# Start places of matmul operands: one fixed pair, or a spread over 32 and 64 places

## The chip, the cores and the metric

The kernel runs on one core of one Trainium2 chip. The time is the device time of one execution in microseconds (us). A core has five engines with queues of their own: TensorE (PE, matmuls; its weight loads are shown apart as PEld), VectorE (DVE), ScalarE (ACT), GpSimd (POOL) and SyncE (SP, which here issues the DMAs). They work out of an on-chip memory of 128 partitions; a place in it is told here in 32-bit words along the partition.

## The reference

One step of a decoder layer, for a prompt of 256 tokens and 8 sequences of 4 new tokens each. The 288 tokens go through the same weights. Three branches (convolution, stick-breaking attention, attention over a memory) are gated, added and projected with `w_o`; then comes the feed-forward part, which is half of the work:

```python
merged = gates[:, :, 0] * y_conv + gates[:, :, 1] * y_sb + gates[:, :, 2] * y_mem
x = x + merged @ p['w_o']                                    # 2048 x 2048
h2 = rms_norm(x, p['g_mlp'])
x = x + jnp.square(jax.nn.relu(h2 @ p['w_up'])) @ p['w_down']   # 2048 x 8192, 8192 x 2048
```

All of it is in 32-bit floats.

## The kernel before

Features lie along the partitions and the 288 tokens along the columns. A product of 32-bit precision is made of three fast ones: each operand is split into a high part, rounded to the format `float32r`, and a low part, the rest. An output tile of 128 features by 288 tokens is the sum, over 16 blocks of 128 input features, of high times high, high times low and low times high: 48 matmuls of 288 columns. The weights are the stationary operand (128 columns, loaded before each matmul) and the activations the moving one.

The weights come in 504 slabs of 128 x 1024 words, one DMA each (L285). ACT rounds a slab into a buffer of the pool `wh` (L307), DVE puts the difference into one of `wl` (L318); both pools have four buffers of 1088 words, 64 more than a slab. `shifted` chooses the column in the buffer at which the slab begins: 0 for the first 16 slabs, 5 (`SHIFT`) for all others. `products` (L538) runs through a slab: first the high weights with the high and the low part of each activation block in turn, then the low weights with the high parts, 24 matmuls. Two slabs make an output tile of a product with 2048 input features; the last 256 slabs are the feed-forward part's.

The activations lie in two kinds of places. `Acts` takes two buffers of 320 words from pool `a`, one for the high and one for the low part, and begins at word 4 (`AHEAD`) in both; `hx`, the input of the first half, and `h2`, the input of `w_up`, are of this kind. The homes (`make_homes`) are cut from ten buffers of pool `k4` of 1024 words, three to a buffer, 320 words (`APART`) from one to the next, and from two buffers of pool `s`: 32 in all, a high and a low one for each of 16 blocks. They begin at word 36 (`HOME`) of their section. `merged`, the input of `w_o`, is in the homes, and then, for each of the four quarters of the feed-forward part, the 16 blocks that `w_up` produces and `w_down` reads. In the compiled program the buffers of `a` begin 16 words past a multiple of 64, and those of `k4`, `s`, `wh` and `wl` 48 past. With the columns above, each moving operand of L538 begins 20 words past a multiple of 64, and its weights 53 past (48 in the first 16 slabs, which L591 multiplies, with the roles exchanged: there the slab is the moving operand, 512 columns at a time). The names of the profile leave out numbers: `k` is `k4`.

The small attention products (`three`, L917 to L919) read operands that begin at the buffers' own first column or a multiple of 128 behind it.

The order of all engines' work is found when the program is built: a planner (`Order`) steps jobs, each with an engine, an estimated time and buffers that it needs, and issues what can start first. A matmul counts as 0.131 us there. In the feed-forward part TensorE runs the tiles of `w_up` (`up_tile`: DVE takes the relu out of the sum, POOL squares, ACT and DVE make the high and the low home) and then those of `w_down` (`down_tile`), for each of the quarters.

Of the kernel before, what the change touches and what calls it, by code (L numbers as in the profile page):

```python
# [8 lines left out]
F32R = mybir.dt.float32r  # L9
# [6 lines left out]
P = 128  # L16
D_MODEL = 2048
KT = D_MODEL // P
# [4 lines left out]
T = NP + NS  # L23
# [14 lines left out]
N_SLABS = 504  # L38
# [37 lines left out]
class Order:  # L76
# [31 lines left out]
    def give(self, pool, n=1):  # L108
        self.pools[pool] += [self.now.ready] * n
# [45 lines left out]
def dve(n, *flags, **take):  # L155
    return Ask("DVE", 0.18 + n / 920.0, flags, **take)


def act(n, *flags, **take):
    return Ask("ACT", 0.22 + n / 1200.0, flags, **take)  # L160


def pool(n, *flags, **take):
    return Ask("POOL", 0.3 + n / 420.0, flags, **take)


def pe(us, *flags, **take):
    return Ask("PE", us, flags, **take)


def sp(*flags, **take):
    return Ask("SP", 0.45, flags, **take)


APART = 320
AHEAD, HOME = 4, 36
PAD = 64
GRP = 32
SHIFT = 5
MM = 0.131  # L180
MM_MEM = 0.226

# [2 lines left out]
def tile_decoder_step(ctx: ExitStack, tc: tile.TileContext, xT, memT, wall, cvec, kmat, ptab,  # L185
# [23 lines left out]
    def tl(p, shape, dt=F32):  # L209
        cnt[0] += 1  # L210
        return pools[p].tile(shape, dt, tag=p, name=f"{p}_{cnt[0]}")
# [48 lines left out]
    def col(c):  # L260
        return cv[:, c:c + 1]
# [9 lines left out]
    class Slab:  # L271
        def __init__(self, parts):
            self.parts = parts
            self.landed = [Flag() for _ in range(parts)]
            self.split = [Flag() for _ in range(parts)]
# [11 lines left out]

    def shifted(p, s):
        n = 0 if s < 2 * KT // 2 else SHIFT
        return tl(p, [P, SLAB + PAD], F32R)[:, n:n + SLAB]  # L290

    def due(s):
# [4 lines left out]
    def cast_weights():  # L297
        todo = [(0, 0), (1, 0), (0, 1), (1, 1)] + [(s, i) for s in range(2, N_SLABS) for i in range(slabs[s].parts)]
        for s, i in todo:
            sl = slabs[s]  # L300
            n = SLAB // sl.parts
            cast_at[0] = s
            yield act(n, sl.landed[i], **({} if i else {"w": 1}))
            if i == 0:
                sl.h = shifted("wh", s)
            c = slice(i * n, (i + 1) * n)
            nc.scalar.copy(sl.h[:, c], sl.raw[:, c])  # L307
            sl.split[i].cast = order.now.ready
            add(sub_part(s, i), lambda s=s: 0 if due(s) - order.free["DVE"] < 5.0 else 4.5)

    def sub_part(s, i):
        sl = slabs[s]
        n = SLAB // sl.parts
        yield dve(n, late=Order.HOP + 0.1)
        if i == 0:
            sl.l = shifted("wl", s)
        c = slice(i * n, (i + 1) * n)
        nc.vector.tensor_sub(sl.l[:, c], sl.raw[:, c], sl.h[:, c].bitcast(F32))  # L318
        done(sl.split[i])
        if i == sl.parts - 1:  # L320
            give("wr")
# [5 lines left out]
    class Acts:  # L327


        def __init__(self, n=T):  # L330
            c = slice(AHEAD, AHEAD + n) if n == T else slice(32, 32 + n)
            self.h, self.l = tl("a", [P, APART], F32R)[:, c], tl("a", [P, APART], F32R)[:, c]
            self.flag = Flag()

    hm, hx = [None] * KT, [None] * KT
# [208 lines left out]
    def products(ps, uses, acts, first=True, last=True, n=T):  # L544
# [6 lines left out]
        for i in range(0, len(todo), STEP):  # L551
            part = todo[i:i + STEP]
            yield pe(len(part) * MM, *sl.split, *{a.flag for _, _, a, _ in part})
            if i == 0 and first:
# [45 lines left out]
    def conv_products(evacs):  # L600
# [8 lines left out]
        for k2, o in turns:  # L609
# [9 lines left out]
            for i in range(2):  # L619
                todo.append((sl.l, slice(i * 512 + o * P, i * 512 + (o + 1) * P), "h", 2 * k2 + i))  # L620
            yield pe(6 * MM, *sl.split, hx_in[2 * k2], hx_in[2 * k2 + 1])
            if o == 0:
# [704 lines left out]
    def make_homes():  # L1327
        yield sp(*conv_done, *osb_in, k4=bufs["k4"], s=bufs["s"])
        parts = []
        for _ in range(bufs["k4"]):  # L1330
            x = tl("k4", [P, 1024], F32R)
            parts += [x[:, HOME + i * APART:HOME + i * APART + T] for i in range(3)]
        for _ in range(bufs["s"]):
            parts.append(tl("s", [P, 512], F32R)[:, HOME:HOME + T])
        for j in range(KT):
            homes.append(Home(parts[2 * j], parts[2 * j + 1]))
        done(homes_in)
# [45 lines left out]
    x1, h2 = [None] * KT, [None] * KT  # L1383
# [4 lines left out]
    def out_tile(j):  # L1388
        res = []
        here = Flag()  # L1390

        def load():
            yield sp(t=1)
            res.append(tl("t", [P, T]))
            nc.sync.dma_start(res[0], xT[:, j, :])
            here.at = order.landed(147) + 1.0

        def evac(ps):
            yield dve(T, here, a=3)
            x = x1[j] = tl("a", [P, T])  # L1400
            nc.vector.tensor_add(x, ps, res[0])
            give("pm")
            a = h2[j] = Acts()
            yield act(T)
            nc.scalar.mul(a.h, x, col(C_GMLP + j))
            yield dve(T)
            nc.vector.scalar_tensor_tensor(a.l, x, col(C_GMLP + j), a.h.bitcast(F32), op0=ALU.mult, op1=ALU.subtract)
            done(h2_in[j])
            a.flag = h2_in[j]
            yield act(T)  # L1410
            if j == 0:
                sq_sum.append(res[0])
            nc.scalar.activation(res[0], x, AF.Square)  # L1413
            if j:
                yield pool(T)
                nc.gpsimd.tensor_add(sq_sum[0], sq_sum[0], res[0])  # L1416
                give("t")
            if j == KT - 1:
                done(sums_2)
        return load, evac  # L1420
# [110 lines left out]
    with tc.manual_schedule():  # L1531
        add(loads(), 1.0)
        add(cast_weights(), lambda: 0 if due(cast_at[0]) - order.free["ACT"] < 6.0 else 4.5)
        add(mem_norm(), 0.6)
        add(x_norm(), 0.6)
        add(main(), 20.0)
        add(conv_norm(), 8.0)
        add(read_pages(), 4.0)
        add(make_homes(), 1.0)
        order.run()  # L1540
# [157 lines left out]
```

## Time and profile before

| what | value |
|---|---|
| time, median of 2 runs | 1616.84 us (1616.59 to 1617.10) |
| the profiled execution | 1617.72 us, its span 1615.9 us |
| TensorE busy, share of the span | 1610.4 us, 100% |
| VectorE, ScalarE, GpSimd busy | 978.3, 752.6, 139.6 us |
| DMA | 310.25 MB, mean 192 GB/s |

The span is from the first instruction of the program to the end of the last. A group of instructions is shown with its line, engine, operation, the tiles it writes and reads (`pm<-a,wh` is a matmul into `pm` with the moving operand from `a` and the weights from `wh`), its count, the total and the mean time of one, and what ended the idle time before it. The chain of waits follows the work that ended last back to the start. A row of a window gives its length, the busy time (and count) of the engines asked for, the granted share of TensorE's clock, and the DMAs' share and rate. Matmuls overlap in their pipeline, so the time of one (292 ns) is not what it costs; the distance from start to start is. A row of the timeline begins with the start in us and the time.

### The profile page before, as it was taken

How to read it: one execution, taken by the hardware profiler on the slowest of the kernel's cores; microseconds unless marked ns; L12 is line 12 of the kernel's file. 1: busy time of each engine (PE TensorE's matmuls, PEld its weight loads, DVE VectorE, ACT ScalarE, POOL GpSimd, SP SyncE). 2: the span in 40 equal slices, each digit the busy share in tenths (PEclk: the TensorE clock that was granted, in tenths of full speed). 3: DMA queues.
4: the chain of work that ended last, by engine and by line, in shares of the span. 5: the costliest groups of instructions: out<-in, count | busy, mean ns of one | idle time of the engine just before them, and what ended most of it. 6: DMA issues, size and time to landing. Idle time of an engine off the chain costs nothing.

```text
span 1615.9 us, 30749 instructions
## 1 busy us (share of the span) xinstructions
PE 1610.4 (100%) x12638; PEld 1592.4 (99%) x12638; DVE 978.3 (61%) x1503; ACT 752.6 (47%) x1078; POOL 139.6 (9%) x106
## 2 busy tenths in 40 slices
PE   9999999999999999999999999999999999999999
PEld 7999999999999999999999999999999999999999
DVE  7889888877777655655555544555445554455443
ACT  8856877654334534444443333333333333333332
POOL 0020000000000000002222100121002210022100
PEclk9999999999999999999999999999999999999999
DMA  9887778987755555466655555555555555555562
GB/s 326 231 198 267 201 256 237 323 225 271 220 170 166 173 169 170 151 195 191 193 171 167 170 170 169 168 170 171 169 170 170 170 170 169 171 167 169 180 194 95
DMA packets 127200, 310.25 MB, mean 192 GB/s; under 512 B 40018, under 2 KB 49618, under 8 KB 127058
## 3 DMA queue, kind: packets, MB, share of 16 engines
q1 hardware_dynamic: 126770, 307.98, 61.2%
q8 instruction: 99, 1.62, 0.4%
q10 hardware_dynamic: 288, 0.29, 0.1%
q14 instruction: 43, 0.35, 0.1%
HBM read 296.99 MB, written 6.32 MB: 188 GB/s over the span
## 4 chain that ended last, share of the span: by engine, by line
PE 97%; DVE 1%; DMA 1%; issue 0%; ACT 0%; SPq 0%; DVEq 0%; ACTq 0%
PE pm L538 91%; PE pm L591 3%; DMA wr<-in_wall 1%; PE pa L538 1%; PE pl L1090 1%; DVE wl L318 1%; PE pl L1274 0%; PE pa L917 0%; PE pa L919 0%; PE pa L918 0%; PE pl L1104 0%; DVE a L770 0%; PE pa L1214 0%; PE pa L1250 0%; ACT wh L307 0%
## 5 line engine op out<-in xcount | busy, mean ns | idle before, releaser
L307 ACT CAST wh<-wr 128x1024 fp32r<-128x1024 f32 (+1 forms) x520 | 529.2, 1022 | 643.3 <-PE pm L538 570.6
L318 DVE TENSOR_TENSOR wl<-wr,wh 128x1024 fp32r<-128x1024 f32 (+1 forms) x520 | 618.2, 1193 | 192.6 <-ACT wh L307 189.6
L538 PE MATMUL pm<-a,wh 128*128 128x288 f32 x5184 | 733.9, 292 | 0.0
L538 PEld LDWEIGHTS pm<-a,wh 128*128 128x128 f32 x5184 | 695.2, 188 | 1.4 <-issue 1.0
L538 PE MATMUL pm<-a,wl 128*128 128x288 f32 x2592 | 394.9, 292 | 0.0
L538 PEld LDWEIGHTS pm<-a,wl 128*128 128x128 f32 x2592 | 358.0, 188 | 0.0
L538 PE MATMUL pm<-k,wh 128*128 128x288 f32 x2400 | 338.0, 292 | 0.0
L538 PEld LDWEIGHTS pm<-k,wh 128*128 128x128 f32 x2400 | 321.6, 188 | 0.0
L538 PE MATMUL pm<-k,wl 128*128 128x288 f32 x1200 | 181.8, 292 | 0.0
L538 PEld LDWEIGHTS pm<-k,wl 128*128 128x128 f32 x1200 | 165.4, 188 | 0.0
L1430 POOL TENSOR_TENSOR t<-t 128x288 f32<-128x288 f32 x64 | 96.7, 1510 | 599.2 <-DVE t L1427 599.2
L1444 DVE TENSOR_TENSOR a<-a,pm 128x288 f32<-128x288 f32 x64 | 29.0, 454 | 122.7 <-PE pm L538 122.7
L1427 DVE SCALAR_TENSOR_TENSOR t<-pm,rx 128x288 f32<-128x288 f32 x64 | 29.3, 457 | 92.1 <-PE pm L538 92.1
L1433 ACT CAST k<-t 128x288 fp32r<-128x288 f32 x60 | 26.0, 433 | 126.0 <-POOL t L1430 126.0
L1346 DVE TENSOR_TENSOR t<-pm,rx 128x288 f32<-128x288 f32 x48 | 22.0, 458 | 71.8 <-PE pm L538 71.8
L1435 DVE TENSOR_TENSOR k<-t,k 128x288 fp32r<-128x288 f32 x60 | 28.0, 466 | 59.4 <-ACT k L1433 59.4
L770 DVE SCALAR_TENSOR_TENSOR a<-a,cv,a 128x256 f32<-128x256 f32 x120 | 59.5, 496 | 1.4
L1416 POOL TENSOR_TENSOR t<-t,t 128x288 f32<-128x288 f32 x15 | 21.9, 1462 | 413.9 <-ACT t L1413 413.9
L591 PE MATMUL pm<-wh,a 128*128 128x512 f32 x128 | 34.8, 392 | 0.5 <-ACT wh L307 0.5
L538 PE MATMUL pm<-s,wh 128*128 128x288 f32 x160 | 33.8, 292 | 0.0
L591 PEld LDWEIGHTS pm<-wh,a 128*128 128x128 f32 x128 | 24.1, 190 | 6.5 <-ACT wh L307 1.6
L538 PEld LDWEIGHTS pm<-s,wh 128*128 128x128 f32 x160 | 25.6, 188 | 0.0
(181 smaller groups left out, 707.7 us busy)
## 6 DMA issues: line engine op xcount, KB each, us to landing
wr<-in_wall SPq DMA_DIRECT2D x488, 512.0 KB, 3.7
wr<-in_wall SPq DMA_DIRECT2D x32, 256.0 KB, 5.1
k<-in_kpool SPq DMA_DIRECT2D x32, 256.0 KB, 5.9
k<-in_vpool SPq DMA_DIRECT2D x32, 256.0 KB, 5.9
k<-in_mkc SPq DMA_DIRECT2D x8, 512.0 KB, 8.9
k<-in_mvc SPq DMA_DIRECT2D x8, 512.0 KB, 8.2
t<-in_xT SPq DMA_DIRECT2D x16, 144.0 KB, 3.7
out_yT<-a SPq DMA_DIRECT2D x16, 144.0 KB, 1.9
```

Source lines behind the costliest of these rows:

```text
L307: nc.scalar.copy(sl.h[:, c], sl.raw[:, c])
L318: nc.vector.tensor_sub(sl.l[:, c], sl.raw[:, c], sl.h[:, c].bitcast(F32))
L538: nc.tensor.matmul(ps, w, a, start=(first and i == 0), stop=(last and i == len(todo) - 1))
L591: nc.tensor.matmul(ps[m], y[:, m * P:(m + 1) * P], z[:, w], start=(k == 0 and j < 2), stop=(k == KT - 1 and j in (4, 5)))
L770: nc.vector.scalar_tensor_tensor(c[:, :NP], up[:, k:k + NP], w, c[:, :NP], op0=ALU.mult, op1=ALU.add)
L1346: nc.vector.tensor_mul(g, ps, rx)
L1416: nc.gpsimd.tensor_add(sq_sum[0], sq_sum[0], res[0])
L1427: nc.vector.scalar_tensor_tensor(r, ps, 0.0, r2, op0=ALU.max, op1=ALU.mult)
L1430: nc.gpsimd.tensor_mul(r, r, r)
L1433: nc.scalar.copy(a.h, r)
L1435: nc.vector.tensor_sub(a.l, r, a.h.bitcast(F32))
L1444: nc.vector.tensor_add(x1[j], x1[j], ps)
```

## The change

Operands of the feed-forward part no longer begin at one common place. The weights of the output tile number 16 c + f (quarter c, tile f, in `w_up` and `w_down` alike) begin at column 27 (16 c + f) mod 64 of their buffers, so that all 64 values occur. The 32 buffers of `h2` begin at 11 i mod 32, with i = 0 to 31 through the high and low parts in turn. The 32 homes begin at (11 i + 32 k) mod 64 of their section, where k is the section's number in its buffer; that gives 32 different places of the 64. The homes hold `merged` too, so that the product with `w_o` reads its moving operand from the new places, with its weights at 5 as before. All else, the other users of `Acts` among it, stays at word 4 and shift 5; no buffer changes its size, and no instruction is added or taken away.

```diff
-AHEAD, HOME = 4, 36
+AHEAD, HOME = 4, 0
+FF0 = N_SLABS - 4 * 4 * KT

     def shifted(p, s):
         n = 0 if s < 2 * KT // 2 else SHIFT
+        if s >= FF0:
+            c, i = divmod(s - FF0, 4 * KT)
+            n = 27 * (c * KT + i // 2 % KT) % 64
         return tl(p, [P, SLAB + PAD], F32R)[:, n:n + SLAB]

-        def __init__(self, n=T):
-            c = slice(AHEAD, AHEAD + n) if n == T else slice(32, 32 + n)
-            self.h, self.l = tl("a", [P, APART], F32R)[:, c], tl("a", [P, APART], F32R)[:, c]
+        def __init__(self, n=T, at=(AHEAD, AHEAD)):
+            c, d = (slice(x, x + n) if n == T else slice(32, 32 + n) for x in at)
+            self.h, self.l = tl("a", [P, APART], F32R)[:, c], tl("a", [P, APART], F32R)[:, d]

             x = tl("k4", [P, 1024], F32R)
-            parts += [x[:, HOME + i * APART:HOME + i * APART + T] for i in range(3)]
+            for i in range(3):
+                at = i * APART + (11 * len(parts) + 32 * i) % 64
+                parts.append(x[:, at:at + T])
         for _ in range(bufs["s"]):
-            parts.append(tl("s", [P, 512], F32R)[:, HOME:HOME + T])
+            at = 11 * len(parts) % 64
+            parts.append(tl("s", [P, 512], F32R)[:, at:at + T])

-            a = h2[j] = Acts()
+            a = h2[j] = Acts(at=[11 * (2 * j + x) % 32 for x in range(2)])
```

## The prediction

> **What bounds the kernel now.** I read the page first: its shares of busy time, its row of granted clock, and its chain of waits.
>
> ```profile
> span 1615.9 us, 30749 instructions
> PE 1610.4 (100%) x12638; PEld 1592.4 (99%) x12638; DVE 978.3 (61%) x1503; ACT 752.6 (47%) x1078; POOL 139.6 (9%) x106
> PEclk9999999999999999999999999999999999999999
> PE 97%; DVE 1%; DMA 1%; issue 0%; ACT 0%; SPq 0%; DVEq 0%; ACTq 0%
> PE pm L538 91%; PE pm L591 3%; DMA wr<-in_wall 1%; PE pa L538 1%; PE pl L1090 1%; DVE wl L318 1%; PE pl L1274 0%; PE pa L917 0%; PE pa L919 0%; PE pa L918 0%; PE pl L1104 0%; DVE a L770 0%; PE pa L1214 0%; PE pa L1250 0%; ACT wh L307 0%
> ```
>
> TensorE is on the chain for 97% of the span, and 91% of it is one line, the product loop L538. The clock is granted in full in all slices (a 9 is 90% or more; a row below says 1.00), so the time of this line is a count of matmuls times the spacing of their starts. Next comes the chain in order of time, for its last pieces.
>
> ```profile
> 422.81 3.70 PE pl L1090 x128
> 426.52 1185.81 PE pm L538 x9120
> 1612.33 0.02 issue
> 1612.35 0.46 DVE a L1444
> ```
>
> From 426.5 us to the end nothing interrupts the products: 9120 matmuls in 1185.81 us, 130.02 ns each, for 288 columns. The busy time of this line by stretches says the same: TensorE stands still for 0.69 us out of 1086.50, and the weight loads run beside the matmuls without a gap.
>
> ```profile
> 526.50:1613.00 1086.50, 1085.81 (x8353) 1085.59 (x8351) 1.00 0.54 170
> ```
>
> So the sum has one kind of term: a change in the 130.0 ns, times the matmuls that it concerns. The other engines stand off this chain, which the groups by line and shape show.
>
> ```profile
> L318 DVE TENSOR_TENSOR wl<-wr,wh 128x1024 fp32r<-128x1024 f32 x488 | 597.3, 1226 | 190.1 <-ACT wh L307 187.2 <-ACT t L1413 1.5 <-DVE t L461 0.4
> L307 ACT CAST wh<-wr 128x1024 fp32r<-128x1024 f32 x488 | 510.8, 1048 | 638.9 <-PE pm L538 570.6 <-issue 29.0 <-DMA wr<-in_wall 20.9
> L318 DVE TENSOR_TENSOR wl<-wr,wh 128x512 fp32r<-128x512 f32 x32 | 21.0, 686 | 2.5 <-ACT wh L307 2.3
> L307 ACT CAST wh<-wr 128x512 fp32r<-128x512 f32 x32 | 18.4, 612 | 4.5 <-DMA wr<-in_wall 4.2
> L538 PEld LDWEIGHTS pm<-a,wh 128*128 128x128 f32 x5184 | 695.2, 188 | 1.4 <-issue 1.0 <-ACT s L986 0.4
> L591 PEld LDWEIGHTS pm<-wh,a 128*128 128x128 f32 x128 | 24.1, 190 | 6.5 <-ACT wh L307 1.6
> ```
>
> ACT, which makes each weight slab's high part, waits 570.6 us for TensorE to free a buffer: it is the one that is early.
>
> **What the change touches.** It adds, removes and reorders no instruction, wait or transfer. The planner's costs stay, so the order stays; the buffers keep their sizes, so they keep their addresses. SP's and POOL's queues hold what they held. Only start columns move. Of the instructions that touch them:
>
> The casts and subtractions that write the weights. Before, the first slabs (512 columns at a time) are written at shift 0 and all others (1024) at shift 5. In the rows above 512 more columns cost ACT 1048 − 612 = 436 ns and DVE 1226 − 686 = 540 ns, less than the first 512 with their fixed part, so no dearness of an odd place stands out, and odd the places of the feed-forward weights are already. I set the cost at nothing. Were it 10% either way, it would be 123 ns for a DVE subtraction of 1226 that comes once in 24 × 130.0 = 3120 ns; TensorE hides it, with ACT's wait as the measure of the slack. If that cover were gone, it would be 256 × 0.12 = 31 us.
>
> The small evacuations into h2 and into the homes (64 + 16 on ACT, as many on DVE): the same reasoning, and none ends a wait of TensorE.
>
> The matmuls and weight loads. Feed-forward slabs are 504 − 248 = 256, with 24 matmuls each: 6144, or 799 us of the 1185.81. In them the moving operand and the weights move. In the output product with w_o, 16 tiles of 48 = 768 matmuls read `merged` out of the same homes; there the moving operand alone moves.
>
> **What a place costs.** Before, every product of L538 has the same pair of places: moving operands 20 words past a multiple of 64 (16 + 4 in `a`, 48 + 36 in the homes), weights 53 past (48 + 5). Their difference is 33. So the trace has the price of one pair out of the 32 × 64, and for others I go to matmuls on other lines. In the memory products (L591) both operands stand at 48, a difference of 0, with 512 columns. In the attention products of 256 columns two kinds stand: `pa<-a,a`, both at 16 (difference 0), and `pa<-s,a`, moving at 48 and weights at 16 (difference 32). The chain from 10 to 50 us, and the timeline at two such groups, the matmul behind each included:
>
> ```profile
> 9.94 40.12 PE pm L591 x177
> ```
>
> ```profile
> 157.27 0.28 PE L917 MATMUL pa<-a,a 128*128 128x256 f32 x1
> ...
> 157.86 0.28 PE L919 MATMUL pa<-a,a 128*128 128x256 f32 x1
> 157.98 0.30 PE L538 MATMUL pm<-a,wh 128*128 128x288 f32 x1
> ```
>
> ```profile
> 177.51 0.28 PE L917 MATMUL pa<-s,a 128*128 128x256 f32 x1
> ...
> 178.35 0.28 PE L918 MATMUL pa<-s,a 128*128 128x256 f32 x1
> 178.47 0.28 PE L919 MATMUL pa<-s,a 128*128 128x256 f32 x1
> 178.59 0.27 PE L1250 MATMUL pa<-s,a 128*128 128x128 f32 x1
> ```
>
> The first gives 40.12 / 177 = 226.7 ns for 512 columns. The second has six matmuls from 157.27 to 157.98: 118.3 ns. The third has nine from 177.51 to 178.59: 120.0 ns. Starts are rounded to 10 ns, so these two are good to 1.7 and 1.1 ns. At difference 0 a column costs (226.7 − 118.3) / 256 = 0.423 ns. For 288 columns that makes 118.3 + 32 × 0.423 = 131.8 ns at difference 0, and 120.0 + 13.5 = 133.5 ns at difference 32. The pair of now, at 130.0, is the cheapest of the three, by 1.8 and 3.5 ns.
>
> The change replaces this one pair by a spread over all of them. The mean of the three known prices is 131.8, 1.8 ns over now. I take 1.5 ns, a little less, because pairs as odd as the present one come up often among the new ones and the two dear ones both begin on round places. The bounds: above, all at 133.5, +3.5 ns. Below, a matmul that costs its columns alone, 288 × 0.423 = 121.8 ns, −8.2 ns; no row comes near it, so I stay by the rows at 256 and 512 columns.
>
> Sum: feed-forward 6144 × 1.5 ns = 9.2 us; w_o 768 × 0.75 ns = 0.6 us (one operand moved, so half). Together +9.8 us. On the profiled execution's 1617.7 us (1615.9 of span and 1.8 around it) that is 1627.5 us; the median of the runs lies 0.9 lower at 1616.84, so 1627 us rounded. With the upper bound it is 6912 × 3.5 = 24 us, 1641 us.
>
> [...]
>
> **The rivals.** No effect: the difference between the two groups of 256 columns is rounding or their surroundings, and 130.0 is what 288 columns cost anywhere. For it: all of the 9120 matmuls keep 130.0 although their buffers lie all over the memory, with DVE, ACT and DMA busy beside them. Against: 226.7 for 512 columns and 130.0 for 288 leave 96.7 for 224 columns, 0.432 each, and then 256 columns would cost 130.0 − 13.8 = 116.2, where both groups are above. Time: 1617 us.
>
> Faster: the present pair is itself a bad one, and the spread averages it away. The most that is in it is 6912 × 8.2 = 57 us, 1560 us; halfway to that floor it is 28 us, 1589 us. For it: between 130.0 and 121.8 there are 8.2 ns in each matmul that no column accounts for. Against: no place of the trace has less of it (118.3 − 108.3 = 10.0 at 256 columns, 226.7 − 216.6 = 10.1 at 512).
>
> Slower by over 2%: a moving operand that begins off a multiple of four words. All moving operands of L538 begin on one now (20); after, the low parts all begin at odd places and of the high parts every second begins two words off, so of three products in a group two are concerned, 4608 of 6912. The trace has no such product. The weights do begin off it, at 53, and their loading takes 188 ns where the aligned weights of L591 take 190; a moving operand may still suffer, since it has no slack. Price: from nothing up to a column's time for each of its 72 groups of four words, 72 × 0.423 = 30.5 ns. It decides from 32.3 us on, 7.0 ns for each of the 4608; with 9 ns it is 41 us, 1658 us; with all 30.5 it would be 1757 us. No place in the rows costs more than 3.5 ns over now, half of those 7.0, so its chance is small. [...]
>
> **How the numbers follow.** Forecast, slower by a little (1618.5 to 1641 us): 0.46. No effect: 0.22. Faster: 0.18, two thirds of it within 2%, because a floor that all places miss will hardly be reached by a mean over places. Slower by over 2%: 0.14. The bound of 2%, about what a measurement can tell here, is 32.3 us, or 1584.5 and 1649.2 us. So faster 0.06, same 0.46 + 0.22 + 0.12 = 0.80, slower 0.14. The range should leave out no more than 0.2: below, the 0.06 and a part of the faster cases, and above, all but the nearest of the slower rival. So it goes from 1600 (−2.4 ns for each matmul) to 1652 us (+5.1 ns). The likeliest case by itself has 1618.5 to 1641.
>
> **What would show it.** The chain must still end in one unbroken piece of L538 with 9120 matmuls; its length over 9120 minus 130.02 is the change itself: 131.1 for +9.8 us. Two rows bound the stages, the first home that TensorE reads, by the instructions of L538, and the first matmul of the feed-forward part, in the timeline:
>
> ```profile
> L538 PE MATMUL pm<-k,wh x2400: 290/292/294, 713.6 to 1610.7; 128*128 128x288 f32 x185
> ```
>
> ```profile
> 813.43 2.24 PE L538 MATMUL pm<-a,wh 128*128 128x288 f32 x16
> ```
>
> Up to 713.6 us the traces must agree. From 813.4 us the spacing should vary from output tile to output tile, since each of 64 tile places has its own weights' place; if it is flat at 130.0, no effect has won. If instead it follows the moving operand, low parts dearer than high ones, the slower rival has. The casts must stay near 1048 and 1226 ns, and ACT's wait for TensorE must not fall. Wrong in another way would be a TensorE that now waits for wh or wl, or a granted clock below full.

## The result and the profile after

The changed kernel takes 1640.08 us (1639.96 to 1640.20) where the kernel before takes 1616.84: 1.0144 times as long, with a 95% interval of 1.0128 to 1.0160. It is slower by 23.2 us, 2.4 times the 9.8 us of the forecast, and inside the range given.

The page of the profiled execution (1639.96 us), its busy shares, its clock and the start of its chain of waits:

```profile
span 1638.2 us, 30749 instructions
PE 1633.0 (100%) x12638; PEld 1615.9 (99%) x12638; DVE 980.4 (60%) x1503; ACT 753.0 (46%) x1078; POOL 139.5 (9%) x106
PEclk9999999999999999999999999999999999999999
PE 97%; DVE 1%; DMA 1%; ACT 1%; issue 0%; SPq 0%; DVEq 0%; ACTq 0%
```

The same instructions, the same clock, and TensorE as unbroken as before; VectorE's and ScalarE's busy times have moved by 2.1 and 0.4 us, off the chain. (The line numbers of the changed kernel are four higher: L542 is L538.) The chain in order of time, its last pieces:

```profile
421.54 3.70 PE pl L1094 x128
425.24 1209.42 PE pm L542 x9120
1634.68 0.45 DVE a L1451
```

This piece was 1185.81 us for the same 9120 matmuls. It has grown by 23.61 us and begins 1.3 us sooner, at 425.24 instead of 426.52; the two together are the 22.3 us by which the profiled span has grown. Cut into stages, the chain gives the spacing, a stretch's length by its count:

```profile
720.00 90.07 PE pm L542 x672
```

```profile
819.97 780.06 PE pm L542 x5851
```

The first stretch lies in the product with w_o: 90.07 / 672 = 134.0 ns. The second lies in the feed-forward part: 780.06 / 5851 = 133.3 ns. Both were 130.0. Within the feed-forward part the output tiles differ, from 132.2 to 134.7 ns by the starts of their matmuls, as the prediction said that they should. So 768 x 4.0 = 3.1 us come from w_o and 6144 x 3.3 = 20.5 us from the feed-forward part, 23.6 in all. The groups by line and shape show the writers untouched by the new places:

```profile
L322 DVE TENSOR_TENSOR wl<-wr,wh 128x1024 fp32r<-128x1024 f32 x488 | 598.4, 1228 | 193.5 <-ACT wh L311 190.6 <-ACT t L1420 1.6 <-DVE t L465 0.4
L311 ACT CAST wh<-wr 128x1024 fp32r<-128x1024 f32 x488 | 510.7, 1048 | 661.5 <-PE pm L542 594.7 <-issue 30.3 <-DMA wr<-in_wall 24.4
```

1228 and 1048 ns, 1226 and 1048 before; and ACT waits 594.7 us for TensorE instead of 570.6, longer by what TensorE lost.

One thing in this did not fit my picture: w_o, where only the moving operand moved, lost more for each matmul than the feed-forward part, where both did. My first theory came from there: that a matmul pays when its moving operand begins at another place than the one before it (A). Against it stood that each pair of places has a price (B), and that the weights' move is what costs (C).

### The profile page after: what moved, and what is told of

Read it like the earlier page. It is cut to its first block, busy times and chain, and to the rows that moved or that the text cites. A ratio compares the mean times of both kernels' runs of the same rounds, so it can differ in the third digit from the quotient of the medians.

```text
span 1638.2 us, 30749 instructions
## 1 busy us (share of the span) xinstructions
PE 1633.0 (100%) x12638; PEld 1615.9 (99%) x12638; DVE 980.4 (60%) x1503; ACT 753.0 (46%) x1078; POOL 139.5 (9%) x106
## 4 chain that ended last, share of the span: by engine, by line
PE 97%; DVE 1%; DMA 1%; ACT 1%; issue 0%; SPq 0%; DVEq 0%; ACTq 0%
PE pm L542 91%; PE pm L595 3%; PE pa L542 1%; DMA wr<-in_wall 1%; PE pl L1094 1%; DVE wl L322 1%; PE pl L1278 0%; ACT wh L311 0%; PE pa L921 0%; PE pa L923 0%; PE pa L922 0%; PE pl L1108 0%; DMA a<-in_hist 0%; DVE a L774 0%; ACT a L696 0%
## 5 line engine op out<-in xcount | busy, mean ns | idle before, releaser
L311 ACT CAST wh<-wr 128x1024 fp32r<-128x1024 f32 (+1 forms) x520 | 529.4, 1022 | 666.0 <-PE pm L542 594.7
L542 PE MATMUL pm<-a,wh 128*128 128x288 f32 x5184 | 740.6, 294 | 0.0
L542 PEld LDWEIGHTS pm<-a,wh 128*128 128x128 f32 x5184 | 701.2, 188 | 1.4 <-issue 1.4
L542 PE MATMUL pm<-a,wl 128*128 128x288 f32 x2592 | 398.3, 293 | 0.0
L542 PEld LDWEIGHTS pm<-a,wl 128*128 128x128 f32 x2592 | 361.0, 188 | 0.0
L542 PE MATMUL pm<-k,wh 128*128 128x288 f32 x2400 | 346.6, 296 | 0.0
L542 PEld LDWEIGHTS pm<-k,wh 128*128 128x128 f32 x2400 | 329.5, 189 | 0.0
L542 PE MATMUL pm<-k,wl 128*128 128x288 f32 x1200 | 186.0, 296 | 0.0
L542 PEld LDWEIGHTS pm<-k,wl 128*128 128x128 f32 x1200 | 169.0, 189 | 0.0
L1440 ACT CAST k<-t 128x288 fp32r<-128x288 f32 x60 | 26.0, 433 | 127.6 <-POOL t L1437 127.6
L542 PE MATMUL pm<-s,wh 128*128 128x288 f32 x160 | 34.4, 296 | 0.0
L542 PEld LDWEIGHTS pm<-s,wh 128*128 128x128 f32 x160 | 25.7, 188 | 0.0
```

The source lines that it names most:

```text
L542: nc.tensor.matmul(ps, w, a, start=(first and i == 0), stop=(last and i == len(todo) - 1))
L1440: nc.scalar.copy(a.h, r)
```

## The experiments

A number given as the spacing at a place is the time from one matmul's start to the next one's. A pair is written (moving place, weights' place), in words past a multiple of 64. A time without an interval is that of a single execution. The diffs show the lines that carry the change; `...` stands for lines left out.

**One part alone.** The first keeps the new weights' places and takes the moving ones back; the second does the reverse. Both start from the changed kernel.

```diff
-AHEAD, HOME = 4, 0
+AHEAD, HOME = 4, 36
...
-            for i in range(3):
-                at = i * APART + (11 * len(parts) + 32 * i) % 64
-                parts.append(x[:, at:at + T])
+            parts += [x[:, HOME + i * APART:HOME + i * APART + T] for i in range(3)]
-            at = 11 * len(parts) % 64
-            parts.append(tl("s", [P, 512], F32R)[:, at:at + T])
+            parts.append(tl("s", [P, 512], F32R)[:, HOME:HOME + T])
...
-            a = h2[j] = Acts(at=[11 * (2 * j + x) % 32 for x in range(2)])
+            a = h2[j] = Acts()
```

> The weights of the feed-forward part are spread over the 64 places as in the change; all moving operands stay at 20 past a multiple of 64. Theory A (a matmul costs more when its moving operand begins at another place than the one before it; the weights' place is free): 130.0 ns everywhere, 1617 us. Rival B (each pair of places has its price, and the pair before is a cheap one): the product with w_o back at 130.0 ns, the feed-forward part still near 133.3, so 1617 + 20 = 1637 us, with tiles that differ from each other. Rival C (moving the weights is what costs): as B, 1637 us, all tiles alike.

```diff
-        if s >= FF0:
-            c, i = divmod(s - FF0, 4 * KT)
-            n = 27 * (c * KT + i // 2 % KT) % 64
```

> h2 and the homes are spread as in the change; all weights of the feed-forward part stay at shift 5. Theory A (steps between moving operands cost): 133 to 134 ns in the product with w_o and in the feed-forward part, 1640 us. Rival B (price of a pair): about the same, since the pairs still vary, 1635 to 1642 us. Rival C (moving the weights costs): only the product with w_o stays dear, 768 x 4.0 ns = 3 us, 1620 us.

Measured: weights alone 1628.68 us, ratio 1.0074 (1.0057 to 1.0091); moving operands alone 1640.70 us, ratio 1.0148 (1.0131 to 1.0165). The last piece of the chain, of the first kernel and of the second:

```profile
425.09 1198.09 PE pm L542 x9120
```

```profile
424.90 1210.24 PE pm L539 x9120
```

Over 1185.81 that is 12.28 us for the weights, 24.43 for the moving operands, and 23.61 for both together. The parts don't add: each spread by itself leaves the cheap pair of before, and once it is left, spreading the other operand too brings nothing more. A falls as the only cause with the first run, since its moving operands never step and yet it loses 12 us. C falls with the second. B stands, though not with the size that was expected of it: it had 133.3 ns and 1637 us for the weights alone, which cost 132.0 and 1628.68. Within the first run it can be seen at work, because there all matmuls of an output tile share one pair. Three tiles of it, by the chain, with the weights 8, 35 and 51 past a multiple of 64:

```profile
862.56 6.11 PE pm L542 x47
```

```profile
868.68 6.52 PE pm L542 x48
```

```profile
1476.56 6.34 PE pm L542 x47
```

130.0, 135.8 and 134.9 ns. Grouping all starts of this run by the weights' place in the compiled program, the 64 places have a mean of 132.0 ns and reach from 130.0 to 136.0 (the differences of neighbouring starts, averaged within a tile; the 135.8 above counts one matmul of the tile before); about one place in six has the 130.0 that the kernel before had.

**Fixed pairs, a quarter each.** With the moving operands at 20 as before and from the kernel of the first run:

```diff
-            n = 27 * (c * KT + i // 2 % KT) % 64
+            n = (0, 36, 4, 21)[c]
```

> Moving operands at 20 past a multiple of 64, as before; the weights at one fixed shift in each quarter of the feed-forward part: 0, 36, 4, 21, which stand 28, 0, 32 and 49 words past the moving operand's place (33 before). Theory A (steps between moving operands cost): 130.0 ns in every quarter, 1617 us. Rival B (price of a pair): the quarter at difference 0 at 131.8 ns and the one at 32 at 133.5, by the attention and memory products, the others between 130 and 134; by the two alone 1536 x (1.8 + 3.5) = 8 us, 1625 us or more.

Measured: 1629.17 us. The chain in the four quarters:

```profile
814.88 195.22 PE pm L542 x1489
```

```profile
1014.95 195.08 PE pm L542 x1493
```

```profile
1217.94 197.07 PE pm L542 x1478
```

```profile
1419.94 195.07 PE pm L542 x1463
```

131.1, 130.7, 133.3 and 133.3 ns in turn: the spacing goes by the fixed pair. The third, at the difference of 32 words, is near where the prediction put it (133.5); the second, at 0, is not (131.8). A, which had 130.0 in all four, falls here too.

**Two moving places.** The weights at shift 5 throughout:

```diff
-AHEAD, HOME = 4, 36
+AHEAD, HOME = 4, 0
...
-            a = h2[j] = Acts()
+            a = h2[j] = Acts(at=(4, 15))
```

> Weights at shift 5 throughout. In h2 all high parts begin at word 4 and all low parts at word 15; the homes all begin at word 0, that is 48 past a multiple of 64 where it was 20. Theory A (steps between moving operands cost): the tiles of w_up step in 16 of 24 matmuls (high, low, high, low; then high alone), so 130.0 + 2/3 x 3.3 = 132.2 ns there, 3072 x 2.2 = 7 us; the tiles of w_down and w_o at one place, though a new one, 130.0; 1624 us. Rival B (price of a pair): w_down and w_o at another pair, up to 133.5 ns, 3840 x 3.5 = 13 us; w_up dear in its low parts alone, one matmul in three; up to 1633 us, and the dear stage is w_down.

Measured: 1635.36 us. In order of time w_o, w_up and w_down:

```profile
719.91 90.13 PE pm L539 x676
```

```profile
815.90 99.24 PE pm L539 x752
```

```profile
917.91 97.20 PE pm L539 x729
```

133.3, 132.0 and 133.3 ns. A gave 130.0 for the first and the last, which hold one moving place all the time; they are the dear ones, as B had it. The new pair (48, 53) costs 3.3 ns more than (20, 53) for no other reason than its place. But w_up speaks for A, which had 132.2 there. Two of its three products have their moving operand at 20, which costs 130.0 when it is held; by B alone the third, at 31, would have to cost 136.0 to make 132.0. The run with other rows, below, holds the pair (31, 53) for one tile:

```profile
1111.27 5.98 PE pm L543 x46
```

That is 130.0 ns. So both places are cheap when held, and going back and forth between them costs 2.0 ns a matmul on average. Both B and a price of stepping are at work.

**Other rows.** From the first run's kernel, the weights still spread, each stage with one moving place of its own. The homes of a quarter are cut from the same buffers at that quarter's word.

```diff
+PLACES = (0, 8, 13, 22, 32)
...
+        for c in range(5):
+            for j in range(KT):
+                at = PLACES[c]
+                homes.append(Home(*(x[:, at:at + T] for x in parts[2 * j:2 * j + 2])))
...
-            a = h2[j] = Acts()
+            a = h2[j] = Acts(at=(15, 15))
```

> Weights spread over the 64 places as in the change; moving operands at one place per stage, each a new one: h2 at word 15 (31 past a multiple of 64), the homes of the four quarters at words 0, 8, 13 and 22 (48, 56, 61 and 6 past), merged at 32. Theory B1 (each pair of places has a price; the mean over all is the 133.3 ns of the change, and 20 with its 132.0 was a cheap row): these rows average 133.3 ns or more, 6144 x 3.3 = 20 us, 1637 us. Theory B2 (pairs average about 132.0 in any row, and 1.3 ns more come from stepping from one moving place to another): 132.0 +- 0.5 in every row, 6144 x 2.0 = 12 us, 1629 us.

Measured: 1631.62 us. The chain in the first w_up (moving at 31), then in the four w_down (48, 56, 61, 6):

```profile
816.00 96.08 PE pm L543 x737
```

```profile
916.90 97.21 PE pm L543 x732
```

```profile
1119.87 96.19 PE pm L543 x725
```

```profile
1320.88 98.18 PE pm L543 x727
```

```profile
1525.96 94.08 PE pm L543 x705
```

130.4, 132.8, 132.7, 135.1 and 133.4 ns. Neither expectation had this: the rows are neither all at 133.3 nor all at 132.0, they differ by 4.7 ns. With the row of 20 at 132.0 they average 132.7, 0.6 below the change. (A w_down row meets only the 16 weights' places of its quarter; at 20 the four sets of 16 cost 131.6 to 132.5, so the sets alone don't make the 4.7.) The dearest tile of the run has the pair (61, 33):

```profile
1339.00 6.34 PE pm L543 x46
```

137.8 ns. The order suggested the rest of the moving place modulo 4 words: 31 leaves 3, then 20, 48 and 56 leave 0, 6 leaves 2, 61 leaves 1.

**Half of the weights.** The spacing of 130.0 ns is 8.2 ns over the columns' own time by the prediction's estimate of 121.8, which it worked out from the spacings at 256 and 512 columns (118.3 and 226.7 ns). If this excess were the weights' reads in the way of the moving ones (D), half the weights should halve it: with 121.8, 125.9, 127.6, 128.9 and 125.9 ns in the four quarters. If it were the moving operand's own reading, or a fixed price of a change of weights (E), the half products should cost what the whole ones do, 130.0, 133.3, 136.0 and 130.0 as these pairs did in the first run.

```diff
+            n = (5, 20, 51, 7)[c]
...
-        todo = high + low
+        todo = high[:-1] + low + high[-1:] if s >= FF0 else high + low
...
+            for j, (w, c, a, x) in enumerate(part, i):
+                n = P // 2 if w is sl.l and s >= FF0 else P
+                nc.tensor.matmul(ps[:n], w[:, c:c + n], a.l if x else a.h, ...)
```

> Moving operands at 20 past a multiple of 64 as before; weights at one shift per quarter: 5, 20, 51, 7 (places 53, 4, 35, 55), which in the run with the weights spread cost 130.0, 133.3, 136.0 and 130.0 ns. In the feed-forward part the low weights' products load and multiply only 64 of their 128 columns (so half of the low products' rows is left out); they stand between the high ones in an unbroken row of 8. [...]

Measured: 1623.04 us. The timeline in the first quarter (weights at 53) and in the second (4), where `128*64` is the half load:

```profile
830.40 1.20 PE L562 MATMUL pm<-a,wl 128*64 128x288 f32 x8
831.44 2.24 PE L562 MATMUL pm<-a,wh 128*128 128x288 f32 x16
833.52 0.68 PE L562 MATMUL pm<-a,wl 128*64 128x288 f32 x4
```

```profile
1109.71 1.22 PE L562 MATMUL pm<-a,wl 128*64 128x288 f32 x8
1110.77 2.29 PE L562 MATMUL pm<-a,wh 128*128 128x288 f32 x16
1112.89 0.82 PE L562 MATMUL pm<-a,wl 128*64 128x288 f32 x5
```

From start to start, 8 half products take 1.04 us, 130 ns each, and the 16 whole ones behind them 2.08, 130 ns too. In the second quarter it is 1.06 and 2.12 us, 132.5 ns for both, with starts rounded to 10 ns; over the whole quarter the starts give 131.5 for the half products and 132.6 for the whole ones. Theory D asks for 125.9 and 127.6. The third quarter behind its first tile (weights at 35) and most of the fourth (55):

```profile
1229.93 170.09 PE pm L562 x1301
```

```profile
1419.91 180.15 PE pm L562 x1377
```

130.7 and 130.8 ns. By kind, from the starts, it is 129.9 for half and 131.3 for whole products in the third quarter, where D asks for 128.9, and 132.4 and 130.0 in the fourth, where the half products are the dearer ones and D asks for 125.9. D falls: half of the weights to read does not halve the excess. E does not come out either: it had both kinds alike at 130.0, 133.3, 136.0 and 130.0, and only the first quarter is so. The price of the third pair, 136.0, came back in the whole products for the first tile alone, as two rows of whole products in it and in the next tile show, each with the row behind it:

```profile
1218.70 2.34 PE L562 MATMUL pm<-a,wh 128*128 128x288 f32 x16
1220.87 1.20 PE L562 MATMUL pm<-a,wl 128*64 128x288 f32 x8
1221.91 2.26 PE L562 MATMUL pm<-a,wh 128*128 128x288 f32 x16
1224.01 1.20 PE L562 MATMUL pm<-a,wl 128*64 128x288 f32 x8
```

16 of them take 2.17 us, 135.6 ns each, and then 2.10 us, 131.3. The run under "Has a pair one price?" takes that up; the two tiles that its expectation speaks of are the two slabs of this one.

**The rest modulo 4.** The change as it is, with each moving place rounded; the second run has `+ 1` for `+ 3`.

```diff
-                at = i * APART + (11 * len(parts) + 32 * i) % 64
+                at = i * APART + (11 * len(parts) + 32 * i) % 64 // 4 * 4 + 3
...
-            at = 11 * len(parts) % 64
+            at = 11 * len(parts) % 64 // 4 * 4 + 3
...
-            a = h2[j] = Acts(at=[11 * (2 * j + x) % 32 for x in range(2)])
+            a = h2[j] = Acts(at=[11 * (2 * j + x) % 32 // 4 * 4 + 3 for x in range(2)])
```

> The change as it is, but each moving place rounded to 3 past a multiple of 4 words (h2 and homes alike); they still step from one matmul to the next, over 8 and 16 places, and the weights still spread over 64. Theory F (the price goes by the moving place's rest modulo 4: 3 is cheap, then 0, 2, and 1 dear; stepping is free): like the row at place 31, 130.5 ns, in the feed-forward part and w_o, 6912 x 0.5 = 3.5 us, 1620 us. Rival G (stepping between moving places costs, whatever the places): 132.5 to 133.5 ns as in the change, 1634 to 1641 us.

> The same with each moving place rounded to 1 past a multiple of 4 words. Theory F (rest modulo 4 decides): like the row at place 61, 135.1 ns, 6912 x 5.1 = 35 us, 1652 us. Rival G (stepping costs, whatever the places): 133.3 ns, 1640 us as the change.

Measured: rest 3, 1625.88 us, ratio 1.0052 (1.0037 to 1.0067); rest 1, 1654.56 us, ratio 1.0231 (1.0216 to 1.0247). The feed-forward part of each:

```profile
819.97 780.11 PE pm L542 x5943
```

```profile
819.95 780.16 PE pm L542 x5761
```

131.3 and 135.4 ns. Two words' difference in where the moving operands begin is worth 29 us, and the kernel with rest 1 is the one that loses more than 2%. G, which had 133.3 for both whatever the places, falls in this form; F has the order and the second size, while the first is 0.8 ns above the 130.5 that it had from the row of 31.

**More rows with rest 3.** As in the run with other rows, with these words:

```diff
+PLACES = (3, 7, 19, 31, 23)
...
+            a = h2[j] = Acts(at=(7, 7))
```

> Weights spread over 64 places; moving operands at one place per stage, all 3 past a multiple of 4: h2 at word 7 (23 past a multiple of 64), the homes of the quarters at words 3, 7, 19 and 31 (51, 55, 3 and 15 past), merged at 23. Theory F (rest modulo 4 decides): every one of these rows averages near the 130.5 ns of place 31, 6912 x 0.5 = 3.5 us, 1620 us. Rival B1 alone (rows differ with no such order): rows anywhere from 130.5 to 135 ns, by their mean of 132.8 about 1636 us.

Measured: 1623.19 us. The first w_up (moving at 23), then the w_down at 51, 55, 3 and 15:

```profile
815.88 94.16 PE pm L543 x723
```

```profile
914.88 95.12 PE pm L543 x721
```

```profile
1115.99 96.11 PE pm L543 x735
```

```profile
1316.89 97.15 PE pm L543 x734
```

```profile
1517.99 97.10 PE pm L543 x744
```

130.2, 131.9, 130.8, 132.4 and 130.5 ns. F had about 130.5 in every row, which two of them miss. The rows at 23, 55, 15 (and 31) leave 7 modulo 8, those at 51 and 3 leave 3, dearer by 1.7 on average. To see whether modulo 8 was the rest that counts, the change was rounded once more, with `// 8 * 8 + 7` in the three places:

> The change as it is, with each moving place rounded to 7 past a multiple of 8 words; they step over 4 and 8 places, the weights spread over 64. So far rows at 7 past a multiple of 8 (15, 23, 31, 55) averaged 130.5 to 130.7 ns, rows at 3 past (3, 51) 131.9 to 132.3, and the run of both mixed 131.3. Theory F8 (the rest modulo 8 decides, stepping is free): 130.6 ns, 6912 x 0.6 = 4 us, 1621 us. Rival G (stepping adds a cost of its own): 131.3 ns as in the mixed run, 1626 us.

Measured: 1625.26 us, ratio 1.0048 (1.0032 to 1.0065), and in the feed-forward part

```profile
820.00 780.12 PE pm L542 x5950
```

131.1 ns. That is hardly better than rest 3 modulo 4 and 0.6 ns above the rows that it is made of (130.5 on average), so here G has a share: about 0.6 ns is tied to the places changing from matmul to matmul. Between 20 and 31 it was 2.0 ns, so what a step costs goes by the places too. Modulo 8 orders the rows that are held, and does not carry over to the spread.

**Has a pair one price?** From the first run's kernel:

```diff
-            n = 27 * (c * KT + i // 2 % KT) % 64
+            n = (51, 7, 51, 3)[c]
```

> Moving operands at 20 past a multiple of 64, the weights at one shift per quarter: 51, 7, 51, 3 (places 35, 55, 35, 51), whole products. With the weights spread these places cost 136.0, 130.0, 136.0 and 134.9 ns for a tile each; where half of the low products was left out, place 35 cost 136.2 ns in two tiles and then 131.1. Theory B1 (a pair has one price): 136.0, 130.0, 136.0, 134.9 ns; 1536 x (6.0 + 0 + 6.0 + 4.9) = 26 us, 1643 us. Rival H (the spacing of a pair depends on what went before): the two quarters at 51 differ, or change within the quarter, between 131 and 136; 1620 to 1643 us.

Measured: 1628.15 us. The chain in the four quarters:

```profile
814.99 195.09 PE pm L542 x1488
```

```profile
1015.97 194.09 PE pm L542 x1493
```

```profile
1215.93 194.17 PE pm L542 x1481
```

```profile
1419.93 190.08 PE pm L542 x1408
```

131.1, 130.0, 131.1 and 135.0 ns. The weights at 55 and 51 cost what they cost before (130.0, 134.9). At 35 they cost 131.1 on average over each of the two quarters, where both tiles of the first run had 136.0. The first run itself has another such pair: (20, 48) took 131.1 ns in its w_up tile and 130.0 in its w_down tile, by the starts; and (20, 35) changed over within one kernel, from 135.6 to 131.3 ns, where half of the low weights was left out. So the same pair can run at more than one spacing; B holds with that restriction. H is right in that (20, 35) does not keep its price from kernel to kernel; within this run the two quarters agree. What sets one spacing or the other isn't shown.

**A better pair.** In the run with other rows the moving place 31 had a few weights' places below 130: 129.3 ns at 2, 5, 54, 57, 60 and 63, in the tiles that hold them. The kernel before with one of them:

```diff
-AHEAD, HOME = 4, 36
+AHEAD, HOME = 15, 47
...
-SHIFT = 5
+SHIFT = 12
```

> The kernel before with another fixed pair for all products of L538: moving operands 31 past a multiple of 64 (words 15 in a and 47 in the homes), weights 60 past (shift 12). Theory B1 (each pair has its price): 129.35 ns as this pair had in the run with other rows, against 130.0: 11,500 matmuls x 0.65 = 7.5 us less, 1609 us. Rival H (a pair's spacing depends on what went before it, and was met there for one tile at a time): anything from 129.3 to 131.7, 1609 to 1636 us, with stretches at different spacings.

Measured: 1609.58 us, ratio 0.9955 (0.9941 to 0.9968): faster than both kernels. The last piece of its chain:

```profile
424.28 1179.73 PE pm L538 x9120
```

129.4 ns on average, without a break; from 819.98 us on, 6032 of them take 780.14 us, 129.3 ns each. It is what the tile prices promised.

## Why the prediction was wrong

The direction and the place were right, and the time lies inside the range; the size was not.

- **What bounds the kernel** was right: one unbroken row of 9120 matmuls. Its length makes the whole difference, 23.61 us in the profiled executions, of which 1.3 come back by its sooner start.
- **The writers and the queues at nothing** was right: 1048 and 1228 ns, and ACT's wait rose with TensorE's time.
- **"The mean of the three known prices is 131.8 ... I take 1.5, a little less"** is the step that failed: the term 6144 x 1.5 ns = 9.2 us measured 6144 x 3.3 ns = 20.5 us. Three prices were too few for pairs that the runs show to reach from 129.3 to 137.8 ns, and the sum had no term for stepping from place to place. The reason given for going below the mean, that odd places are as good as the present one, was wrong: 130.0 is the floor of its row, held by about one weights' place in six, and other rows are dearer. Had I gone by the upper bound, all at 133.5, the sum would have been 1641; that this is so near is luck. Its 133.5 came from one group of the trace before, and another group with the same operands, by its first row and the row behind it, takes 0.71 us for six matmuls, 118.3 ns, the same as at difference 0 and good to 1.7 ns:

```profile
198.85 0.28 PE L917 MATMUL pa<-s,a 128*128 128x256 f32 x1
...
199.56 0.30 PE L538 MATMUL pm<-a,wh 128*128 128x288 f32 x1
```

- **"768 x 0.75 ns (one operand moved, so half)"** failed too, at 4.0 ns measured. The moving operand is the one that matters more: moving operands alone lose 24.43 us of the chain, as much as both, and weights alone 12.28.
- **The difference of the two places** as what sets the price was assumed silently, when 256 columns at (48, 16) stood in for 32 words and those at (16, 16) for 0. At difference 5, (48, 53) costs 133.3 and (20, 25), in its tiles of the first run, 132.0. At difference 0, (20, 20) costs 130.7, but (48, 48), held for a tile in the run with other rows, 131.7:

```profile
915.19 6.06 PE pm L543 x46
```

For (48, 48), which the memory products have, the prediction's carrying over to 288 columns (131.8) fits; giving that price to every pair at the same difference was not. The moving place counts for itself.
- **The rival "no effect"** is out: with the moving operand held at 20, the weights' place alone moves the spacing from 130.0 ns (at 55) to 135.0 (at 51), and with the weights held at 53 the moving place alone moves it from 130.0 (at 20) to 133.3 (at 48).
- **The rival "slower by over 2%"** had something right and its mechanism wrong. The rest modulo four words of the moving place does matter, but the order is not aligned against unaligned: rest 3 is cheapest (131.3 with all places spread), rest 0 stands in the middle (132.0 to 132.8 in its rows), then rest 2 (133.4, one row), and rest 1 is dearest (135.4 with all places spread). In the change low parts begin at rests 1 and 3 by turns, and high parts at 0 and 2, so that it averages them: low (135.4 + 131.3) / 2 = 133.3, high (132.5 + 133.4) / 2 = 133.0, which makes 133.1 against 133.3 measured. This sum was made afterwards and mixes spread and held places, so it is no proof. The sign that the prediction gave for this rival, low parts dearer than high ones, is not seen: by the starts in the changed kernel the two are within 0.4 ns.

What stays open is the mechanism: why the rest of the moving place counts as it does, why one pair can run at two spacings, how much of the change's 3.3 ns is stepping and how much the pairs' own prices, and what the 7.5 ns are that even the best pair (129.3) has over the 121.8 estimated for its columns from the spacings at 256 and 512 columns. Matmuls without a weight load, and other column counts at the same pairs, were not tried.

## What to carry to other kernels

Where a row of back-to-back matmuls is the whole bound, the start columns of both operands can matter with nothing else changed: here they were worth from 0.5% less to 2.3% more time. They are a thing to search over, not to spread. One spread run with the spacing read tile by tile prices 64 pairs at once, and the best of them can then be held throughout; here that took the kernel from 1616.9 to 1609.6 us. The price of a tile is a hint and not a promise, as (20, 35) shows with 136.0 ns in one kernel and 131.1 in another, so a pair has to be measured where it is held. A price seen at one pair says little about the mean over others, so a forecast for a spread should lean to the dear side of what is known when the present pair is the cheapest of it.

## What the runs showed of the hardware that was not expected

- The start column of the moving operand, within four words, is worth 4.1 ns in 130 (131.3 at rest 3, 135.4 at rest 1).
- Going back and forth between two moving places costs by itself: 20 and 31 took 130.0 ns each when held (weights at 53) and 132.0 by turns.
- Held pairs differ in their spacing, averaged over long rows: 129.4 ns over 9120 matmuls with (31, 60), 130.0 over 9120 with (20, 53), 130.7 over 1493 with (20, 20), 131.1 over 1489 with (20, 48), 133.3 over 1478 with (20, 52) and over 1463 with (20, 5), 135.0 over 1408 with (20, 51).
- The same pair can run at more than one spacing: moving at 20 and weights at 35 took 136.0 ns in one kernel, 131.1 in another, and went from 135.6 to 131.3 within a third.
- Matmuls that load and multiply 64 weight columns instead of 128 had a spacing of 129.9 to 132.4 ns in the four quarters, beside 130.0 to 132.6 for whole ones.
